# Expert dots of five blocks split between VectorE and ScalarE, a two-pass output projection, and one more row buffer for block 2, on one Trainium2 core

## The chip, the cores and the metric

The kernel runs on one core of a Trainium2 chip: TensorE for matrix products, VectorE and ScalarE for elementwise work, GpSimd, which here only issues gathers, and SyncE, which issues the plain DMAs. The metric is the time of one launch on the device in microseconds. The kernel before takes 3988.34 us, the median of 3 runs from 3983.55 to 3989.04.

## The reference, cut to what matters

One block of a model over 1024 tokens of width 1024, all in float32: a norm, two token mixers (chunked retention and RWKV-7) that are gated, merged and projected by `w_o`, then PEER, a layer of 16384 experts of which every token picks 128, then a gated embedding and a last norm.

```
merged = sigmoid(gate_ret) * branch_ret + sigmoid(gate_rwkv) * branch_rwkv
x  = x + merged @ w_o
h2 = rmsnorm(x, g_ffn)
q  = h2 @ w_pq                      # per head two halves; scores against 128 sub-keys each
ids, gates = top 16 of the sums of the two top-16 lists, for each of 8 heads
act = gelu(sum over d of h2[t, d] * expert_u[ids[t, k], d])      # the "dots"
x  = x + sum over k of gates[t, k] * act[t, k] * expert_v[ids[t, k]]
```

## The kernel before, in words

The 1024 tokens are 8 blocks of 128. The phases have letters, which stand at the start of every name in the profile: M (branches), O (output projection), N (second norm), F (queries and scores), S (choice of the experts), D (dots), K and W (weights for the values), V (values), G (values by gathering), L (the last layer). The number behind the letter is the block, or, for M, O, N and F, a unit of tokens: unit 2 is the last 512 tokens, blocks 4 to 7.

**Dots (D), `dots`, L930 to L972.** For each of a block's 128 choices GpSimd gathers one row of `expert_u` for each token, a tile of 128x1024 floats (L954), and VectorE multiplies it in place with `h2` and sums it, in one instruction with an accumulator (L956). The tile comes from a ring (`row`, L975). Blocks 0 to 2 have `nu` = 3 tiles; from block 3 on `nmore` = 3 tiles of the pool `um` come beside them, 6 in all. A gather waits until the instruction that used its tile last has ended.

**Values.** Blocks 0 to 5 don't gather `expert_v`: all of `expert_v` is streamed through TensorE twice (units V0 and V1, three blocks each), against a matrix of weights M that is built from the choices. A group of 16 tokens of M takes one-hot tiles A (on ScalarE, L1122 and L1123, or on VectorE, L1115, in turn) and B (VectorE, L1128 and L1131), products on TensorE (L1085) and a copy on ScalarE (L1087). Half of the experts (k = 0, then k = 1) is built at a time, 24 groups; the groups of the next half are built beside the stream of the present one. Blocks 6 and 7 gather rows of `expert_v` (L1000), which VectorE adds up (L1002); these take tiles of the same ring.

**Output projection and norm of unit 2 (O2, N2).** `w_out` (L754) loads `w_o` in 16 pieces, four for each quarter of the columns, and multiplies them with all four blocks. `norm2` (L777) takes the four blocks one after the other: sum of squares on ScalarE (L314), a row tile of which there is one (its weights loaded by L788, its product on VectorE by L789, its store by L790), and a scaling (L791). Only then do transposes (L795) and the split into two tiles (L797, L798) follow, and F2.

**Order.** The whole program is written as a list of phases (`order` and `later` in `cfg`, L862). A scheduler turns it into one fixed list of instructions for each engine, with waits by semaphores; it orders by program order and by its own estimate of when things are ready. So an engine that waits for one instruction holds back all that stands behind it, and a change at one place can move instructions of other phases.

## Time and profile before

| | |
|---|---|
| median of 3 runs | 3988.34 us (3983.55 to 3989.04) |
| the profiled execution | 3982.74 us, span 3980.8 us |
| busy, share of the span | TensorE 86%, VectorE 75%, GpSimd 39%, ScalarE 27% |
| granted TensorE clock, mean | 0.922 of 2.4 GHz |
| HBM | 1055.87 MB moved, 265 GB/s in the mean |

The busy shares are means over stages of different kinds. Up to some 1640 us mixers, projections and the dots of blocks 0 and 1 alternate. From there to 2100 us unit 2 is projected, normed and scored while the rows of block 2 come in. From 2100 to 3810 us the dots of blocks 3 to 7, the values and their weights run side by side, and the last 171 us are the last layer. "Granted clock" is the share of TensorE's full speed that the throttle allowed; DMA share is the mean busy share of the 16 DMA engines.

### The profile page before, as it was taken

Reading aid. Unit: us, or ns where it says so; the run is one execution under the profiler, and the core shown is the slowest. Engines: PE = TensorE matmul, PEld = TensorE weight load, DVE = VectorE, ACT = ScalarE, POOL = GpSimd, SP = SyncE. Lnnn points to the kernel's source line nnn. Section 1 sums busy time; section 2 is a strip of 40 time slices with the busy share of each in tenths; the row PEclk is TensorE's granted clock in tenths of the full one; section 3 lists DMA queues with packets and bytes.
Section 4 is the critical chain, followed back from the end, with each engine's and each line's share of the span. In section 5 each row is a group of like instructions: output and inputs, shape, how many; then the busy total and the mean of one; then the engine's idle time right before and its main releaser. Section 6 shows DMA issues by size and latency. Waiting matters only on the chain.

```text
span 3980.8 us, 53073 instructions
## 1 busy us (share of the span) xinstructions
PE 3431.2 (86%) x18323; PEld 2516.6 (63%) x18323; DVE 2974.2 (75%) x7197; ACT 1062.5 (27%) x2232; POOL 1545.5 (39%) x1288
## 2 busy tenths in 40 slices
PE   6997758997899998948568989489898999799988
PEld 6886647887888887536454445366775555466643
DVE  5663487886777764876788999989877898867733
ACT  4432342221232213013371024310732222200022
POOL 0000013223333200044426568765066676777700
PEclk9998879998999999979768999699998999899999
DMA  6336558778777627488849999899399999999941
GB/s 193 111 95 195 170 164 258 224 240 268 243 252 244 210 77 246 139 282 284 277 149 350 413 345 368 305 360 382 115 335 372 380 390 380 370 403 407 407 157 51
DMA packets 499394, 1055.87 MB, mean 265 GB/s; under 512 B 41074, under 2 KB 279220, under 8 KB 499124
## 3 DMA queue, kind: packets, MB, share of 16 engines
q0 software_dynamic: 184320, 671.17, 46.6%
q1 hardware_dynamic: 314804, 381.31, 28.3%
q8 instruction: 144, 2.36, 0.2%
q14 instruction: 126, 1.03, 0.1%
HBM read 990.58 MB, written 61.73 MB: 264 GB/s over the span
## 4 chain that ended last, share of the span: by engine, by line
issue 19%; DMA 13%; POOL 12%; DVE 9%; PE 8%; ACT 0%; SPq 0%; POOLq 0%; DVEq 0%; ACTq 0%
DMA G6.u<-in_peer_v_dram,D6.u_ids 2%; POOL D7.u L954 2%; DMA G7.u<-in_peer_v_dram,D7.u_ids 2%; DMA D2.u<-in_peer_u_dram,D2.u_ids 2%; POOL D6.u L954 2%; DMA D3.u<-in_peer_u_dram,D3.u_ids 2%; POOL D2.u L954 2%; POOL G7.u L1000 2%; POOL D4.u L954 2%; DVE D3.u L956 2%; DVE D5.u L956 2%; POOL G6.u L1000 2%; DMA D5.u<-in_peer_u_dram,D5.u_ids 1%; PE D5.acc L1163 1%; PE W1.pw L1085 1%
## 5 line engine op out<-in xcount | busy, mean ns | idle before, releaser
L1163 PE MATMUL D5.acc<-V0.v,M.M 128*128 128x512 f32 x1536 | 695.1, 610 | 2.4 <-ACT M.M L1087 1.8
L1163 PE MATMUL D7.acc<-V1.v,M.M 128*128 128x512 f32 x1536 | 669.1, 598 | 11.1 <-DMA V1.v<-in_peer_v_dram 11.1
L1163 PEld LDWEIGHTS D7.acc<-V1.v,M.M 128*128 128x128 f32 x1536 | 373.1, 244 | 298.2 <-issue 185.0
L1163 PEld LDWEIGHTS D5.acc<-V0.v,M.M 128*128 128x128 f32 x1536 | 372.6, 247 | 270.9 <-issue 173.0
L954 POOL DMA_INDIRECT D0.u<-in_peer_u_dram,D0.u_ids x128 | 132.4, 1035 | 829.9 <-DMA D0.u_ids<-idsd 542.3
L954 POOL DMA_INDIRECT D2.u<-in_peer_u_dram,D2.u_ids x128 | 137.7, 1076 | 527.5 <-DVE S3.ti L846 302.9
L1085 PEld LDWEIGHTS <-W0.A 128*128 128x128 bf16 x2304 | 153.8, 138 | 188.4 <-issue 115.9
L954 POOL DMA_INDIRECT D1.u<-in_peer_u_dram,D1.u_ids x128 | 136.0, 1063 | 249.6 <-DVE D1.u L956 152.6
L954 POOL DMA_INDIRECT D6.u<-in_peer_u_dram,D6.u_ids x128 | 163.4, 1277 | 177.2 <-DVE S7.m L887 80.0
L956 DVE SCALAR_TENSOR_TENSOR D2.u<-D2.u,D2.u_h 128x1024 f32<-128x1024 f32 x128 | 156.4, 1223 | 86.8 <-DMA D2.u<-in_peer_u_dram,D2.u_ids 86.1
L1085 PE MATMUL W0.pw<-W0.B,W0.A 128*128 128x64 bf16 x1920 | 133.9, 242 | 96.0 <-DVE W0.B L1131 76.4
L1002 DVE SCALAR_TENSOR_TENSOR G7.u_x<-G7.u,D7.u_t,G7.u_x 128x1024 f32<-128x1024 f32 x128 | 164.7, 1287 | 54.9 <-DMA G7.u<-in_peer_v_dram,D7.u_ids 46.6
L954 POOL DMA_INDIRECT D4.u<-in_peer_u_dram,D4.u_ids x128 | 182.3, 1424 | 56.2 <-issue 32.6
L1087 ACT COPY M.M<-W1.pw 128x512 f32<-128x512 f32 x96 | 80.4, 838 | 447.2 <-PE W1.pw L1085 447.2
L956 DVE SCALAR_TENSOR_TENSOR D0.u<-D0.u,D0.u_h 128x1024 f32<-128x1024 f32 x128 | 155.9, 1221 | 56.3 <-DMA D0.u<-in_peer_u_dram,D0.u_ids 54.4
L954 POOL DMA_INDIRECT D3.u<-in_peer_u_dram,D3.u_ids x128 | 142.6, 1114 | 140.8 <-DVE D3.u L956 61.4
L956 DVE SCALAR_TENSOR_TENSOR D1.u<-D1.u,D1.u_h 128x1024 f32<-128x1024 f32 x128 | 156.1, 1222 | 54.3 <-DMA D1.u<-in_peer_u_dram,D1.u_ids 52.7
L956 DVE SCALAR_TENSOR_TENSOR D7.u<-D7.u,D7.u_h 128x1024 f32<-128x1024 f32 x128 | 155.8, 1224 | 54.4 <-DMA D7.u<-in_peer_u_dram,D7.u_ids 47.9
L954 POOL DMA_INDIRECT D7.u<-in_peer_u_dram,D7.u_ids x128 | 168.4, 1316 | 60.6 <-issue 31.7
L956 DVE SCALAR_TENSOR_TENSOR D6.u<-D6.u,D6.u_h 128x1024 f32<-128x1024 f32 x128 | 155.3, 1225 | 47.2 <-DMA D6.u<-in_peer_u_dram,D6.u_ids 46.2
L1000 POOL DMA_INDIRECT G7.u<-in_peer_v_dram,D7.u_ids x128 | 168.5, 1317 | 53.4 <-issue 28.3
L954 POOL DMA_INDIRECT D5.u<-in_peer_u_dram,D5.u_ids x128 | 156.0, 1219 | 80.7 <-issue 18.9
(2267 smaller groups left out, 8452.4 us busy)
## 6 DMA issues: line engine op xcount, KB each, us to landing
V0.v<-in_peer_v_dram SPq DMA_DIRECT2D x128, 512.0 KB
V1.v<-in_peer_v_dram SPq DMA_DIRECT2D x128, 512.0 KB
zsd<-Pw256.stage SPq DMA_DIRECT2D x48, 192.0 KB
Pr0.raw<-in_w_in_dram SPq DMA_DIRECT2D x32, 256.0 KB
Pg0.raw<-in_w_in_dram SPq DMA_DIRECT2D x32, 256.0 KB
F0.raw<-in_w_pq_dram SPq DMA_DIRECT2D x32, 256.0 KB
Pr256.raw<-in_w_in_dram SPq DMA_DIRECT2D x32, 256.0 KB
Pg256.raw<-in_w_in_dram SPq DMA_DIRECT2D x32, 256.0 KB
```

The costliest lines, as they stand in the source:

```text
L954: nc.gpsimd.indirect_dma_start(out=u, out_offset=None, in_=table, in_offset=bass.IndirectOffsetOnAxis(ap=ids[:, k:k + 1], axis=0))
L956: V.scalar_tensor_tensor(u, u, 1.0, h2, op0=ALU.mult, op1=ALU.mult, accum_out=act[:, k:k + 1])
L1000: nc.gpsimd.indirect_dma_start(out=u, out_offset=None, in_=table, in_offset=bass.IndirectOffsetOnAxis(ap=ids[:, k:k + 1], axis=0))
L1002: V.scalar_tensor_tensor(x, u, t[:, k:k + 1], x, op0=ALU.mult, op1=ALU.add)
L1085: nc.tensor.matmul(pw[:, t * 64:t * 64 + 64], At[:, h * 8 + t], B[:, part, h * 2 + t // 4, :, t % 4], start=(part == 0), stop=(part == 2))
L1087: nc.scalar.copy(self.order(tl, k)[:, tt], pw.rearrange("p (t i) -> p t i", t=8))
L1163: nc.tensor.matmul(acc[tb][h], w, v[:, h * 512:h * 512 + 512], start=(k == 0 and s == 0 and m == 0), stop=False)
```

## The change

Three things, of which the diff below shows the core.

- From block 3 on (`wideb` = 3) a row is multiplied by `h2` in place on VectorE (new L969), and ScalarE copies the product in place with an accumulator that gives the sum (new L970). Blocks 0 to 2 keep the one instruction.
- For unit 2 `w_out` runs in two passes of 256 tokens, each of which loads all of `w_o`, so 32 pieces are loaded in place of 16. `norm2` transposes and splits two blocks at a time, as soon as both are scaled.
- The ring becomes a list of pools: 3 tiles, one tile (`nmid`) that is opened with the weights' first pool, and thus in time for block 2, and 2 tiles (`nmore`). Block 2 has 4 tiles, blocks 3 to 7 have 6, as before.

```
     def w_out(self, u, mT):
+        xs = []
+        for b0 in range(0, self.cfg["mf"][u][1], T):
+            xs += self.w_out_pass(u, mT[:, :, b0:b0 + T], b0)
+        return xs
+
+    def w_out_pass(self, u, mT, b0):
...
-        t0, n = self.cfg["mf"][u]
+        t0, n = self.cfg["mf"][u][0] + b0, T
...
             V.tensor_scalar(xs[tb], xs[tb], r, None, op0=ALU.mult)
-        for kc in range(8):
-            pt = self.mm()[:, :n]
-            for tb in range(n // 128):
-                nc.tensor.transpose(pt[:, tb * 128:(tb + 1) * 128], xs[tb][:, kc * 128:(kc + 1) * 128], self.ident)
-            g = self.v("g_ffn", kc)
-            nc.scalar.activation(hT[0][:, kc, :], pt, AF.Copy, scale=g)
-            V.scalar_tensor_tensor(hT[1][:, kc, :], pt, g, hT[0][:, kc, :], op0=ALU.mult, op1=ALU.subtract)
+            if tb % 2:
+                tt = slice(tb * 128 - 128, tb * 128 + 128)
+                for kc in range(8):
+                    pt = self.mm()[:, :T]
+                    for j in range(2):
+                        nc.tensor.transpose(pt[:, j * 128:j * 128 + 128], xs[tb - 1 + j][:, kc * 128:kc * 128 + 128],
+                                            self.ident)
+                    g = self.v("g_ffn", kc)
+                    nc.scalar.activation(hT[0][:, kc, tt], pt, AF.Copy, scale=g)
+                    V.scalar_tensor_tensor(hT[1][:, kc, tt], pt, g, hT[0][:, kc, tt], op0=ALU.mult, op1=ALU.subtract)
...
-               wp2=(512, 4, 3), nu=3, nab=3, lag=1, aact=(1, 2), wide=1, hp=(), nmore=3, lb=2, nk=4,
+               wp2=(512, 4, 3), nu=3, nab=3, lag=1, aact=(1, 2), wide=1, hp=(), nmid=1, nmore=2, wideb=3, lb=2, nk=4,
...
-            V.scalar_tensor_tensor(u, u, 1.0, h2, op0=ALU.mult, op1=ALU.mult, accum_out=act[:, k:k + 1])
+            if b < self.cfg["wideb"]:
+                V.scalar_tensor_tensor(u, u, 1.0, h2, op0=ALU.mult, op1=ALU.mult, accum_out=act[:, k:k + 1])
+            else:
+                V.tensor_mul(u, u, h2)
+                nc.scalar.activation(u, u, AF.Copy, accum_out=act[:, k:k + 1])
...
-        more = self.cfg["nmore"] if self.um else 0
-        if k % (self.nu + more) < self.nu:
-            return self.up.tile([P, D], F32, tag="u", name=self.nm("u"), bufs=self.nu)
-        return self.um.tile([P, D], F32, tag="u", name=self.nm("u"), bufs=more)
+        k %= sum(n for _, n in self.places)
+        for pool, n in self.places:
+            if k < n:
+                return pool.tile([P, D], F32, tag="u", name=self.nm("u"), bufs=n)
+            k -= n
...
+        self.places.append((wc.enter_context(self.tc.tile_pool(name="ux", bufs=1, side="right")), self.cfg["nmid"]))
```

The scheduler then orders all engines anew. Three places of its lists matter here.

ScalarE's list in the middle of block 4, first before. W0.A are the one-hot tiles of the weights (x13: 13 instructions alike), W0.pw the products that are copied into M, D4.u the rows of block 4.

```order
L1122 ACTIVATE W0.A_21599<-cpers,K0.neg_17117 128x128 x13
L1123 ACTIVATE W0.A_21599<-W0.A_21599 128x2048
L1087 COPY M.M_17719<-W0.pw_21623 128x512
L1087 COPY M.M_17719<-W0.pw_21649 128x512
L1087 COPY M.M_15600<-W0.pw_21683 128x512
L1122 ACTIVATE W0.A_21735<-cpers,K2.neg_18281 128x128 x2
L1087 COPY M.M_15600<-W0.pw_21709 128x512
```

The same stretch of ScalarE's list now.

```order
L1137 ACTIVATE W0.A_21842<-cpers,K1.neg_17794 128x128
L1102 COPY M.M_15632<-W0.pw_21866 128x512
L970 ACTIVATE D4.u_19946,D4.u_act_19709<-D4.u_19946 128x1024
L1138 ACTIVATE W0.A_21842<-W0.A_21842 128x2048
L970 ACTIVATE D4.u_19950,D4.u_act_19709<-D4.u_19950 128x1024
L970 ACTIVATE D4.u_19954,D4.u_act_19709<-D4.u_19954 128x1024
L970 ACTIVATE D4.u_19958,D4.u_act_19709<-D4.u_19958 128x1024
L970 ACTIVATE D4.u_19962,D4.u_act_19709<-D4.u_19962 128x1024
L1102 COPY M.M_15632<-W0.pw_21892 128x512
L1102 COPY M.M_17777<-W0.pw_21926 128x512
L970 ACTIVATE D4.u_19966,D4.u_act_19709<-D4.u_19966 128x1024
```

The sums of the rows stand between the tiles A and the copies, so a sum waits for the copies ahead of it, which wait for TensorE.

VectorE's list at the end of the output projection of unit 2, first before. O2.x are the four blocks' rows, N2.h the one row tile of the norm, D2.u the rows of block 2, N2.rsq and N2.st small steps of the norm.

```order
L956 SCALAR_TENSOR_TENSOR D2.u_16770,D2.u_act_16715<-D2.u_16770,D2.u_h_3578_16713 128x1024
L789 SCALAR_TENSOR_TENSOR N2.h_3366_15622<-O2.x_3325_15395,N2.st_15608,N2.h_3366_15622 128x1024
L771 TENSOR_TENSOR O2.x_3328_15401<-O2.x_3328_15401,O2.mm_15585 128x256
L791 TENSOR_SCALAR O2.x_3325_15395<-O2.x_3325_15395,N2.st_15608 128x1024
L276 TENSOR_TENSOR F2.wlo_15945<-F2.raw_15943,F2.whi_15944 128x512
```

The first row of the norm now.

```order
L967 SCALAR_TENSOR_TENSOR D2.u_16784,D2.u_act_16774<-D2.u_16784,D2.u_h_3602_16772 128x1024
L778 TENSOR_TENSOR O2.x_3351_15511<-O2.x_3351_15511,O2.mm_15523 128x256
L796 SCALAR_TENSOR_TENSOR N2.h_3382_15657<-O2.x_3325_15395,N2.st_15643,N2.h_3382_15657 128x1024
L329 SCALAR_TENSOR_TENSOR N2.st_15664<-N2.rsq_15667,N2.st_15664 128x1
L967 SCALAR_TENSOR_TENSOR D2.u_16787,D2.u_act_16774<-D2.u_16787,D2.u_h_3602_16772 128x1024
L798 TENSOR_SCALAR O2.x_3325_15395<-O2.x_3325_15395,N2.st_15643 128x1024
L778 TENSOR_TENSOR O2.x_3352_15513<-O2.x_3352_15513,O2.mm_15533 128x256
L326 TENSOR_TENSOR N2.rsq_15667<-N2.st_15664 128x1
```

The first block's row product stood beside the last addition of the projection (L771); now it stands beside the first addition of the second pass (L778), and 7 more additions follow it.

VectorE's list at the end of block 5, first before. S7 is the choice of experts for block 7; sc, tv and ti belong to its first part (top 16 of each half), oh and the names after it to its second.

```order
L956 SCALAR_TENSOR_TENSOR D5.u_20495,D5.u_act_20116<-D5.u_20495,D5.u_h_4154_20114 128x1024
L847 MATCH_REPLACE S7.sc_25205<-S7.tv_25181,S7.sc_25205 128x128
L846 MAX_INDEX S7.ti_25182<-S7.tv_25181,S7.sc_25205 128x8
L956 SCALAR_TENSOR_TENSOR D5.u_20498,D5.u_act_20116<-D5.u_20498,D5.u_h_4154_20114 128x1024
L848 MAX S7.tv_25181<-S7.sc_25205 128x8
L847 MATCH_REPLACE S7.sc_25205<-S7.tv_25181,S7.sc_25205 128x128
```

The last rows of block 5 now.

```order
L969 TENSOR_TENSOR D5.u_20936<-D5.u_20936,D5.u_h_4178_20429 128x1024
L859 MAX_INDEX S7.ti_25625<-S7.tv_25624,S7.sc_25692 128x8
L883 TENSOR_TENSOR S7.oh_25714<-S7.tv_25624 128x8x16
L969 TENSOR_TENSOR D5.u_20940<-D5.u_20940,D5.u_h_4178_20429 128x1024
L883 TENSOR_TENSOR S7.oh_25714<-S7.tv_25624 128x8x16
```

At the last row of block 5 the choice for block 7 is now in its second part; before it was still in its first. Between the first row of block 5 and the last, 33 instructions of S7 stood in the list before and 100 stand there now; between the last row of block 5 and the tenth row of block 6, 133 of S7 and some 15 groups of weights stood before, and 66 and some 12 groups stand there now.

## Rows read from the trace of the kernel before

**Rows 1.** The page: span, and busy time by engine.
```profile
span 3980.8 us, 53073 instructions
PE 3431.2 (86%) x18323; PEld 2516.6 (63%) x18323; DVE 2974.2 (75%) x7197; ACT 1062.5 (27%) x2232; POOL 1545.5 (39%) x1288
```

**Rows 2.** Stretches: length, busy us (instructions) of five engines, clock, DMA share, GB/s.
```profile
1736.00:1787.00 51.00, 7.92 (x32) 6.02 (x33) 35.78 (x84) 12.89 (x27) 21.33 (x17) 0.50 0.88 308
1787.00:1936.00 149.00, 119.02 (x534) 95.78 (x533) 104.20 (x222) 42.93 (x80) 61.92 (x56) 0.90 0.85 272
1936.00:2022.00 86.00, 36.80 (x386) 28.77 (x384) 66.06 (x142) 36.88 (x73) 32.68 (x34) 0.58 0.79 259
...
2100.00:2307.00 207.00, 184.27 (x492) 83.93 (x491) 191.72 (x603) 11.49 (x27) 124.47 (x113) 0.93 0.98 385
2307.00:2543.00 236.00, 199.65 (x1150) 114.40 (x1149) 212.88 (x377) 77.30 (x181) 181.94 (x128) 0.90 0.95 354
...
2784.00:2872.00 88.00, 75.20 (x659) 60.09 (x659) 73.92 (x308) 68.70 (x149) 5.62 (x6) 0.92 0.28 98
2872.00:3121.00 249.00, 235.98 (x1033) 152.52 (x1032) 201.80 (x378) 71.27 (x151) 159.23 (x124) 0.96 0.93 349
...
3575.00:3810.00 235.00, 226.16 (x521) 153.70 (x520) 166.46 (x134) 0.62 (x2) 165.91 (x126) 0.98 1.00 395
```

**Rows 3.** Waits of VectorE and GpSimd, 1736 to 2022 us: total, times, longest.
```profile
DVE D2.u L956 <- DMA D2.u<-in_peer_u_dram,D2.u_ids: 71.9, 65, 3.1
POOL D2.u L954 <- DVE D2.u L956: 134.2, 79, 6.1
```

**Rows 4.** GpSimd's instructions in order of time: gathers of block 2.
```profile
1988.13 0.94 POOL L954 DMA_INDIRECT D2.u<-in_peer_u_dram,D2.u_ids  x1 [1.46 <-DVE D2.u L956]
...
1994.39 0.94 POOL L954 DMA_INDIRECT D2.u<-in_peer_u_dram,D2.u_ids  x1 [1.01 <-DVE D2.u L956]
```

**Rows 5.** SyncE's instructions in order of time: the row tile of the norm.
```profile
1736.48 1.57 SPq L790 DMA_DIRECT2D h2d<-N2.h  x1
...
1751.26 0.34 SPq L790 DMA_DIRECT2D h2d<-N2.h  x1
...
1765.39 0.33 SPq L790 DMA_DIRECT2D h2d<-N2.h  x1
...
1777.15 0.32 SPq L790 DMA_DIRECT2D h2d<-N2.h  x1
```

**Rows 6.** VectorE's instructions in order of time, two rows of block 4.
```profile
2400.62 1.22 DVE L956 SCALAR_TENSOR_TENSOR D4.u<-D4.u,D4.u_h 128x1024 f32<-128x1024 f32 x1
2401.76 0.09 DVE L956 DVE_READ_ACCUMULATOR D4.u<-D4.u,D4.u_h 128x1 f32 x1
2401.76 1.22 DVE L956 SCALAR_TENSOR_TENSOR D4.u<-D4.u,D4.u_h 128x1024 f32<-128x1024 f32 x1
...
2402.90 0.69 DVE L1131 TENSOR_TENSOR W0.B<-W0.one,K0.w 128x1024 bf16<-128x1024 bf16 x1
```

**Rows 7.** Groups: busy us, mean ns, idle before; float32 tiles of 512 and 256 columns.
```profile
L276 DVE TENSOR_TENSOR F2.wlo<-F2.raw,F2.whi 128x512 fp32r<-128x512 f32 x32 | 22.1, 690 | 3.2 <-ACT F2.whi L275 3.1
...
L771 DVE TENSOR_TENSOR O2.x<-O2.x,O2.mm 128x256 f32<-128x256 f32 x16 | 6.7, 422 | 3.5 <-PE O2.mm L296 3.5
```

**Rows 8.** ScalarE's instructions in order of time: a sum of squares.
```profile
1739.25 1.05 ACT L314 ACTIVATE N2.junk<-O2.x 128x1024 bf16<-128x1024 f32 x1
1740.21 0.19 ACT L314 ACTIVATION_READ_ACCUMULATOR N2.junk<-O2.x 128x1 f32 x1
1740.30 0.60 ACT L275 CAST F2.whi<-F2.raw 128x512 fp32r<-128x512 f32 x1
```

**Rows 9.** Waits of ScalarE, first 2307 to 2543 us, then 2872 to 3121 us.
```profile
ACT M.M L1087 <- PE W0.pw L1085: 153.5, 30, 42.1
...
ACT M.M L1087 <- PE W1.pw L1085: 152.5, 15, 37.2
```

**Rows 10.** The page, costliest groups: the stream of the last three blocks' values.
```profile
L1163 PE MATMUL D7.acc<-V1.v,M.M 128*128 128x512 f32 x1536 | 669.1, 598 | 11.1 <-DMA V1.v<-in_peer_v_dram 11.1
```

More of the change, by code (lines that the diff above doesn't have):

```diff
@@ L112, in __init__ @@
         self.kw = {}
-        self.um, self.hT, self.wide = None, {}, 0
+        self.hT, self.wide = {}, 0
         self.ph = "s"
@@ L760, in w_out @@
         for tb in range(n // 128):
-            x = big.tile([P, D], F32, tag=f"x1_{tb}", name=self.nm("x1"))
+            x = big.tile([P, D], F32, tag=f"x1_{b0 // 128 + tb}", name=self.nm("x1"))
             self.q.dma_start(x, self.i["x"][0, t0 + tb * 128:t0 + tb * 128 + 128, :])
@@ L932, in open_dots @@
         self.up = up.enter_context(self.tc.tile_pool(name=self.nm("up"), bufs=1, side="right"))
-        self.nu = n
+        self.places = [(self.up, n)]
         return up
@@ L1019, in open_values @@
         self.vp = e(self.tc.tile_pool(name="vp", bufs=2))
-        if self.cfg["nmore"]:
-            self.um = e(self.tc.tile_pool(name="um", bufs=1))
+        self.places.append((e(self.tc.tile_pool(name="um", bufs=1)), self.cfg["nmore"]))
         self.wide_ctx = ExitStack()
@@ L1224, in last_weights @@
         self.ph = "L"
-        places = [lambda k=k: self.row(k) for k in range(self.nu + self.cfg["nmore"])]
+        places = [lambda k=k: self.row(k) for k in range(sum(n for _, n in self.places))]
         places += [lambda: self.wb.tile([P, D], F32, tag="A", name=self.nm("A"), bufs=self.cfg["nab"])] * 2
```

## The prediction

> **What bounds the kernel now.** I read the page first, then a table of stretches, then who waits in the stretches that the change touches. By the page TensorE is busy for 86% of the span and VectorE for 75%, ScalarE for 27% [rows 1]; no engine is full. The table tells more [rows 2]. From 2100 us on four things are nearly full at once: in block 4 (2307 to 2543 us) VectorE is busy 213 of 236 us, TensorE 200, the DMA engines 95% of the time, and in the last stretch before the tail (3575 to 3810) TensorE 226 of 235 us with the DMA engines at 1.00. So time is lost or won there only where such a stretch starts later or earlier, or in its holes. Two holes stand out. Before 2100 us the rows of block 2 run with three tiles: VectorE waits 71.9 us for rows, and GpSimd 134.2 us for a tile to come free [rows 3]. And from 2784 to 2872 us the DMA engines are at 0.28, since VectorE and ScalarE build weights and choose experts before they take up block 6 [rows 2].
>
> The sums are made against the profiled execution, 3982.74 us (span 3980.8 and 1.9 around it). The median of the three runs, 3988.34, lies 5.6 above it, the lowest 0.8 above; I add 3 at the end.
>
> **The change part by part.**
>
> *Fourth tile for block 2.* A tile's round is a gather, its landing, the product, and the next gather: with three tiles, every third gather starts 1994.39 - 1988.13 = 6.3 us after the one before in the same tile [rows 4], so 2.1 us a row. With four tiles and the same round it would be 1.6 us. VectorE itself needs 1.14 us for a row (start to start) [rows 6] beside its other work. What can be won is what VectorE waits for rows, 71.9 us between 1736 and 2022 us, since behind a waiting row its list also holds back the splits of F2 and the tiles B. What limits it: the DMA engines are at 0.88, 0.85 and 0.79 in these three stretches [rows 2], though at no more than 308 GB/s, where 395 GB/s go through at 1.00 later. Bounds: 0 (no room in the transfers) and -72. I take a little over half: **-40**.
>
> *Projection and norm in halves.* The norm has one row tile, and its four stores start at 1736.5, 1751.3, 1765.4 and 1777.2 us [rows 5], some 13.6 us apart; TensorE is busy only 7.9 of the 51 us until F2 starts [rows 2]. Two of these four rounds now come before the projection's end. All of it would be 2 x 13.6 = 27 us. But VectorE's list still holds 14 rows of block 2 between the last addition and the last split of the norm, where it held 16, so the rows set the pace here, too. From these 51 us I take 15 off, with the rows' own gain in the term above. Against it stand 16 more loads of 256 KB, 4.2 MB, at 308 GB/s 13.6 us of transfers beside a DMA share of 0.88; of these I count 8. Bounds -27 and +14; I take **-7**.
>
> *What the new order moves.* Up to the first row of block 4, 52 more instructions of S4 and S5 stand in VectorE's list after block 2 (31 and 21), and about a group more of the second half's tiles. Work in S steps is short, some 0.2 us each by the spacing of the trace; 52 x 0.2 = 10, and 8 tiles of 0.6 us (0.69 us, as the B in [rows 6], less the overlap with the next) 5: **+15**, on the path, since VectorE is busy 192 of 207 us in block 3. The work comes back at the end of block 5: 67 instructions of S7 (13 us) and 3 of 15 groups of weights stand no longer between block 5 and 6. This hole lasts 88 us, with ScalarE busy 69 of them [rows 2]; 3 of 15 groups are 14 us of ScalarE's 69. S7 hides partly behind it. I take **-17**, bounds -30 and 0, and **+3** for the S7 now between the rows of block 5.
>
> *Product and sum.* On VectorE nothing is won: the accumulator's readout shows 0.09 us, but the next instruction starts at the same moment as the readout, 1.14 us after the row's start [rows 6]. Products of two float32 tiles take 422 ns for 256 columns and 690 for 512 [rows 7], so 1.05 ns a column and, carried on, 690 + 536 = 1226 ns for 1024, where the old instruction takes 1.22 us. If the readout counted after all, 5 x 128 x 0.09 = 58 us of VectorE would go; that is the far end. The Trainium skill (Vector Engine (DVE) Microarchitecture Reference, "Points that are easy to get wrong") says that the old form of instruction runs at half throughput when its two sources lie in SBUF and are not bf16. By that alone the split would halve VectorE's time for a row, an estimate of half a microsecond for each of 640 rows, 320 us. The trace disagrees, since the old instruction on two float32 sources takes no longer than a plain product would [rows 6, 7], and this way gets no chance.
>
> On ScalarE a sum over 1024 columns holds the engine from 1739.25 to 1740.30: 1.05 us [rows 8], 134 us a block. The Trainium skill (Vector Engine (DVE) Microarchitecture Reference, "Points that are easy to get wrong") says that the old instruction runs at half rate when both its sources are in SBUF and not bf16; it would then take over 2.1 us and the split would save a microsecond a row, some 640 us in all. The trace has 1.22 us for two float32 sources and disagrees, so this result gets no chance.
>
> What it costs is a longer round for each tile (one more engine, at least 1.05 us) and ScalarE's list. In block 4 ScalarE is busy 77.3 of 236 us; with 134 it is 211, which leaves 25. In block 6 it is 71.3 + 134 = 205 of 249. And it waits for TensorE's products, 153.5 us in 30 waits in block 4, 152.5 in 15 in block 6 [rows 9]. Such waits cost nothing before; now a row's sum stands behind them, behind the sum the tile, and behind the tile GpSimd's next gather. If a quarter of the waits can't be filled with sums, block 4 takes 211 + 38 = 249 us, 13 more; block 6 stays at 205 + 38 = 243, below its 249, and I put 5 on it; for the longer round in blocks 3, 5 and 7, whose transfers are full anyway, 4 each. Sum **+30**; bounds -58 (readout counted) and +84 (half of the waits stay: 211 + 77 = 288, +52, and 205 + 76 = 281, +32). The Trainium skill (ScalarE: Activation LUTs, "Rules for kernel authors") would leave simple adds and products on VectorE, which speaks against this part. The trace agrees in so far as VectorE gets nothing back for ScalarE's 134 us a block [rows 6, 8]; what following the rule would save is the second rival's price, told below from rows.
>
> Sum: -40 - 7 + 15 - 17 + 3 + 30 = **-16**. 3982.7 - 16 + 3 = **3970 us**, 0.46% below the median. The term for the hole and that for block 2 reach the end because the end is fixed by the rows: after the weights of the last half are done, TensorE streams that half, 669.1/2 = 335 us [rows 10], and the rows of block 7 keep the transfers at 1.00 up to the same moment [rows 2]; a stretch of rows that starts earlier ends earlier.
>
> **The rivals.** A difference under 0.2% (8 us) can't be told from none here: 3980 to 3996 is "same".
>
> - *All of block 2's waits go and the hole shrinks in full*: -72 and -30 in place of -40 and -17: 3925 us. For it: 395 GB/s are possible, 308 are used. Against: the loads of F2 beside the rows. Chance 0.16.
> - *ScalarE's list sets the pace of the rows.* The place is block 4, then 6: copies wait for TensorE, sums behind them, and the ring of six runs dry. Half of the waits left gives +84 in place of the +30, with the rest of it: 3970 + 54 = 4024 us. It decides from the point where ScalarE's part costs over 54 us, which eats up the other terms (-46) and 8 more. For it: 25 us are left free of 236, 153.5 of waits. Against: TensorE has idle time in block 4, so the copies are due soon after the tiles B. Chance 0.25.
> - *The fourth tile is hidden by the transfers*: VectorE's waits go on because the DMA engines are full, 15 in place of 40: 3995 us, no change. For it: shares of 0.79 to 0.88, and 4.2 MB more. Chance 0.15.
>
> **How the numbers follow.** The forecast has 0.44; its own range is 3945 to 3983, of which 0.04 lie in "same". Faster: 0.40 + 0.16 = 0.56. Same: 0.04 + 0.15 = 0.19. Slower: 0.25. The range goes from 3920, below the first rival, to 4015, which holds the milder half of the second: 0.8.
>
> **What would show it.** Right: block 2's last row lands near 1975 us instead of 2021, with VectorE's waits for rows at about half; the product at about 1.22 us and 1.14 from start to start; ScalarE's sum at 1.05; block 4 between 236 and 260 us; the hole before block 6 near 70 us. Wrong: GpSimd waiting for ScalarE by tens of microseconds in blocks 4 and 6, F2 starting no earlier than 1787 us, a hole of 88 us, or block 3 growing by more than 15 us.

## The result, and the profile after

The changed kernel takes 4044.75 us, the median of 4 runs (4041.04 to 4062.50), against 3988.03 for the kernel before in the same comparison: 1.0153 times as long, 95% interval 1.0122 to 1.0185. Forecast were 3970 us, in a range from 3920 to 4015. The profiled execution has a span of 4039.3 us, 58.5 more than before.

The first line of the page's table of busy time (answers to [rows 1]): ScalarE alone has more to do, 1766.6 us against 1062.5; the others are where they were.

```profile
PE 3431.9 (85%) x18323; PEld 2517.9 (62%) x18323; DVE 2969.4 (74%) x6565; ACT 1766.6 (44%) x3520; POOL 1557.6 (39%) x1288
```

Block 2, its gathers and its dots (count, ns min/median/max, first and last start), and the dots before. The last dot starts at 1977.2 us, where it was 2020.5: the fourth tile does its work, and VectorE's wait for rows (total, times, longest) is 46.4 us, where it was 71.9 [rows 3].

```profile
L964 POOL DMA_INDIRECT D2.u<-in_peer_u_dram,D2.u_ids x128: 932/938/1944, 1650.8 to 1971.5; - x128
L967 DVE SCALAR_TENSOR_TENSOR D2.u<-D2.u,D2.u_h x128: 1211/1225/1285, 1681.4 to 1977.2; 128x1024 f32<-128x1024 f32 x128
DVE D2.u L967 <- DMA D2.u<-in_peer_u_dram,D2.u_ids: 46.4, 49, 6.2
...
L956 DVE SCALAR_TENSOR_TENSOR D2.u<-D2.u,D2.u_h x128: 1203/1225/1276, 1681.6 to 2020.5; 128x1024 f32<-128x1024 f32 x128
```

The stretches behind it in the changed kernel, cut at the blocks' ends, with the columns of [rows 2]: the choice of experts and the weights ahead of block 3, blocks 3, 4 and 5, the hole, block 6.

```profile
1979.00:2100.00 121.00, 97.52 (x913) 71.26 (x914) 101.21 (x340) 106.63 (x224) 37.15 (x24) 0.78 0.37 128
2100.00:2309.00 209.00, 174.79 (x430) 77.55 (x429) 184.97 (x426) 132.63 (x238) 131.55 (x105) 0.91 0.95 361
2309.00:2548.00 239.00, 188.03 (x1169) 111.28 (x1168) 213.08 (x253) 213.91 (x439) 164.65 (x129) 0.89 0.93 342
2548.00:2794.00 246.00, 190.50 (x722) 134.61 (x720) 219.47 (x512) 174.07 (x332) 154.33 (x129) 0.88 0.93 349
2794.00:2880.00 86.00, 71.26 (x528) 55.16 (x529) 69.28 (x233) 65.85 (x143) 13.45 (x9) 0.88 0.35 116
2880.00:3157.00 277.00, 239.18 (x1162) 159.61 (x1161) 190.40 (x230) 210.36 (x409) 160.93 (x123) 0.91 0.82 309
```

The 43 us of block 2 are gone by the end of block 3 (2309 against 2307 us). Blocks 4 and 5 are 3 and 5 us longer. The hole is as long as it was (86 against 88 us), and block 6 takes 277 us in place of 249, with the DMA engines at 0.82 in place of 0.93 and the granted clock at 0.91 in place of 0.96, both means between its two levels (0.50 is 1.2 GHz, 1.00 is 2.4) [rows 2].

Who waits there: GpSimd, for ScalarE's sums, in block 3, in block 4, and from the hole to block 6's end (total, times, longest).

```profile
POOL D3.u L964 <- ACT D3.u L970: 142.4, 96, 40.6
...
POOL D4.u L964 <- ACT D4.u L970: 42.6, 51, 2.3
...
POOL D6.u L964 <- ACT D6.u L970: 164.0, 81, 65.0
```

The rows tell only half of it. Cut the same time by what TensorE works on: first the weights of V0 with the stream of its first half, up to the last product of W0; then V0's second half with the first weights of V1; then the rest of V1. Columns as above; first after, then before.

```profile
1994.00:2602.00 608.00, 464.27 (x2670) 267.28 (x2669) 533.99 (x1069) 489.17 (x971) 362.96 (x282) 0.85 0.83 305
2602.00:3053.00 451.00, 399.60 (x1745) 287.37 (x1743) 355.17 (x796) 320.16 (x620) 220.18 (x181) 0.94 0.76 288
3053.00:3870.00 817.00, 759.03 (x2895) 461.11 (x2894) 614.49 (x558) 313.99 (x627) 545.91 (x429) 0.96 0.96 372
```

```profile
2023.00:2602.00 579.00, 481.19 (x2714) 278.46 (x2713) 526.19 (x1249) 182.39 (x410) 371.99 (x290) 0.87 0.87 327
2602.00:3008.00 406.00, 381.88 (x1699) 275.74 (x1699) 348.35 (x1022) 119.72 (x258) 196.71 (x165) 0.97 0.80 300
3008.00:3811.00 803.00, 759.03 (x2896) 460.42 (x2894) 632.98 (x764) 118.77 (x270) 568.32 (x443) 0.97 0.99 388
```

TensorE starts 29 us earlier and needs 29, 45 and 14 us more: 59 us later at the end. In the second and third stretch of before it is busy 382 of 406 and 759 of 803 us; this is the engine that is nearly full from 2602 us to the end. Its waits after, in the first, the second and the third stretch:

```profile
PE W0.pw L1100 <- ACT W0.A L1138: 87.7, 12, 17.7
...
PE K5.pw L1069 <- DMA K5.raw<-wd: 23.1, 1, 23.1
PE W1.pw L1100 <- ACT M.M L1102: 18.2, 3, 6.9
...
PE W1.pw L1100 <- ACT M.M L1102: 41.2, 6, 13.4
```

All of them end on ScalarE or on block 5's late end; before they were 17.7, 12.8, 0.2 and 0 us. They are not all new time, since before TensorE waited for VectorE's tiles B in the first and in the third stretch, and did so for 26.4 and 0 us after:

```profile
PE W0.pw L1085 <- DVE W0.B L1131: 76.4, 26, 13.8
...
PE W1.pw L1085 <- DVE W1.B L1131: 32.7, 2, 22.1
```

### The profile page after: what moved, and what is told of

Its sections match the earlier page's. It is cut to its first block, busy times and chain, and to the rows that moved or that the text cites. A ratio compares the mean times of both kernels' runs of the same rounds, so it can differ in the third digit from the quotient of the medians.

```text
span 4039.3 us, 54176 instructions
## 1 busy us (share of the span) xinstructions
PE 3431.9 (85%) x18323; PEld 2517.9 (62%) x18323; DVE 2969.4 (74%) x6565; ACT 1766.6 (44%) x3520; POOL 1557.6 (39%) x1288
## 3 DMA queue, kind: packets, MB, share of 16 engines
q14 instruction: 135, 1.11, 0.1%
## 4 chain that ended last, share of the span: by engine, by line
issue 20%; POOL 16%; DMA 10%; PE 7%; DVE 5%; ACT 3%; POOLq 0%; SPq 0%; DVEq 0%; ACTq 0%
POOL D3.u L964 3%; POOL D6.u L964 3%; DMA G7.u<-in_peer_v_dram,D7.u_ids 3%; POOL D7.u L964 2%; POOL G6.u L1015 2%; POOL D2.u L964 2%; POOL D4.u L964 2%; DMA G6.u<-in_peer_v_dram,D6.u_ids 1%; POOL G7.u L1015 1%; POOL D5.u L964 1%; PE D5.acc L1178 1%; DMA D4.u<-in_peer_u_dram,D4.u_ids 1%; DMA D2.u<-in_peer_u_dram,D2.u_ids 1%; DMA D5.u<-in_peer_u_dram,D5.u_ids 1%; DMA D6.u<-in_peer_u_dram,D6.u_ids 1%
## 5 line engine op out<-in xcount | busy, mean ns | idle before, releaser
L964 POOL DMA_INDIRECT D6.u<-in_peer_u_dram,D6.u_ids x128 | 172.5, 1347 | 189.5 <-ACT D6.u L970 164.0
L964 POOL DMA_INDIRECT D3.u<-in_peer_u_dram,D3.u_ids x128 | 168.7, 1318 | 160.0 <-ACT D3.u L970 142.4
L969 DVE TENSOR_TENSOR D6.u<-D6.u,D6.u_h 128x1024 f32<-128x1024 f32 x128 | 155.5, 1225 | 85.7 <-DMA D6.u<-in_peer_u_dram,D6.u_ids 78.6
L969 DVE TENSOR_TENSOR D7.u<-D7.u,D7.u_h 128x1024 f32<-128x1024 f32 x128 | 156.0, 1224 | 67.2 <-DMA D7.u<-in_peer_u_dram,D7.u_ids 52.9
L1100 PE MATMUL W1.pw<-W1.B,W1.A 128*128 128x64 bf16 x2304 | 149.9, 243 | 59.7 <-ACT M.M L1102 59.4
L1100 PEld LDWEIGHTS <-W1.A 128*128 128x128 bf16 x2304 | 148.0, 138 | 80.7 <-issue 77.1
L964 POOL DMA_INDIRECT D4.u<-in_peer_u_dram,D4.u_ids x128 | 164.5, 1285 | 75.0 <-ACT D4.u L970 42.6
L964 POOL DMA_INDIRECT D7.u<-in_peer_u_dram,D7.u_ids x128 | 159.1, 1243 | 82.6 <-ACT D7.u L970 56.7
```

The costliest lines, as they stand in the source:

```text
L964: nc.gpsimd.indirect_dma_start(out=u, out_offset=None, in_=table, in_offset=bass.IndirectOffsetOnAxis(ap=ids[:, k:k + 1], axis=0))
L969: V.tensor_mul(u, u, h2)
L1100: nc.tensor.matmul(pw[:, t * 64:t * 64 + 64], At[:, h * 8 + t], B[:, part, h * 2 + t // 4, :, t % 4], start=(part == 0), stop=(part == 2))
```

## The experiments

Ratios are to the kernel before, run beside each group, with 95% intervals. The times of different groups are not compared with each other, only their ratios, and a per cent is 40 us.

**Each part undone or alone.** The split taken back: `wideb=3` becomes

```
wideb=8
```

> The changed kernel with its old instruction for the dots of all eight blocks (product and sum in one on VectorE); fourth tile and halves stay. Theory A: the split alone is what costs; the fourth tile and the halves keep the 43 us by which block 2 ended earlier in the changed kernel (1977 against 2020 us). Then 3988 - 43 = 3945 us, between 3930 and 3960, block 3 again some 211 us in earnest, and nobody waits for ScalarE's sums. Rival B: the new order of the instructions (more of S4 and S5 before block 4) and the halves cost the time; then it stays at 4020 or above, with block 2's early end lost again in block 3.

Measured: 3971.32 us, 0.9972 [0.9954, 0.9990]. Rival B falls: the split is what costs, 1.8% or some 72 us. But theory A's 43 us are not there either; 11 are.

The split alone, in the kernel before:

```
-            V.scalar_tensor_tensor(u, u, 1.0, h2, ..., accum_out=act[:, k:k + 1])
+            if b < 3:
+                V.scalar_tensor_tensor(u, u, 1.0, h2, ..., accum_out=act[:, k:k + 1])
+            else:
+                V.tensor_mul(u, u, h2)
+                nc.scalar.activation(u, u, AF.Copy, accum_out=act[:, k:k + 1])
```

> The kernel before with the split of blocks 3 to 7 alone; three tiles in block 2, projection and norm whole. Theory A: the split costs 57 + 43 = 100 us, so about 4085 us, between 4060 and 4100, with GpSimd waiting for ScalarE over 100 us in blocks 3 and 6. Rival B: 3985 to 4005 us, about as before.

Measured: 4067.17 us, 1.0228 [1.0209, 1.0247]: some 91 of theory A's 100 us, and inside its range. GpSimd waits 131.9 us for ScalarE's sums in block 3 and 159.6 in block 6, as A has it. So the split costs some 20 us more here than beside the other two parts.

The fourth tile taken back: `nmid=1, nmore=2` becomes

```
nmore=3        # and no pool "ux"
```

> The changed kernel without the fourth tile (three tiles in block 2, three more from block 3's end on as before); split and halves stay. Theory A: block 2 ends some 35 to 43 us later again and nothing gives it back: 4080 us, between 4065 and 4095. Rival C: what block 2 wins is lost behind it in any case, because the rows of block 3 wait for the weights of the first half on ScalarE; then it stays within 10 us of 4045.

Measured: 4072.76 us, 1.0254 [1.0231, 1.0277], theory A. So beside the split the fourth tile is worth 40 us with the halves (1.0254 against the changed kernel's 1.0153) and 17 without them (1.0228 for the split alone, 1.0186 in the next run).

Projection and norm whole again (`w_out` and `norm2` of the kernel before; the edit cut to its core):

```
-        for b0 in range(0, self.cfg["mf"][u][1], T):
-            xs += self.w_out_pass(u, mT[:, :, b0:b0 + T], b0)
+        t0, n = self.cfg["mf"][u]       # one pass; the transposes stand behind all four blocks again
```

> The changed kernel with projection and norm of the last 512 tokens whole again; fourth tile and split stay. Theory A: a few us, as the prediction's term of 7: 4045 to 4060 us. Rival: the second read of the projection's weights (4.2 MB) costs more than the earlier norm gives; then 4030 to 4044.

Measured: 4050.89 us, 1.0186 [1.0162, 1.0209]; the changed kernel's interval overlaps. The pairs of runs with and without halves lie up to 0.33% apart, in both signs (-0.33% for this one, +0.26% for the split with three tiles): what the halves are worth stays open, within some 0.3%.

The fourth tile alone in the kernel before, which is the changed kernel with the split and the halves taken back:

```
-  nmore=3
+  nmid=1, nmore=2, wideb=8
```

> The kernel before with the fourth tile for block 2 alone (old instruction throughout, projection and norm whole). With the halves as well it was 0.28% faster than before. Theory A: what block 2 wins is not what TensorE waits for; its tiles B stand still further behind in VectorE's list (row 45 of block 5 for the last group of V0's second half, against 22 before): no change, 3975 to 3990 us. Rival (the rows fix the end): some 30 us faster, 3950.

Measured: 3976.86 us, 0.9986 [0.9963, 1.0008]. No change that can be told, although block 2's dots end 34 us earlier (1986.8 us): theory A.

**What fixes the end.** Half of G7's rows left out of the kernel before:

```
-                self.fetch(128)
+                self.fetch(64)          # and 64 rows in direct() for the last block
```

> The kernel before with 64 of the 128 rows of the last direct gather, G7 (the last block's output lacks half of its sum). Theory A: TensorE's list fixes the end, since it was busy 226 of 235 us beside G7: only the 9 us in which it idled there, 8 to 11 us of waits for V1's tiles, can go: 3970 us, within 8. Rival, the prediction's step (the end is fixed by the rows): 64 x 1.7 us earlier, bounded by the last tiles of V1: 3900 us or below.

Measured: 3974.81 us, 0.9989 [0.9970, 1.0007]. 64 rows less, and the time stays. TensorE's stream of V1 hardly moves, where G7's last addition starts 116 us earlier. First before, then with half of the rows:

```profile
L1163 PE MATMUL D7.acc<-V1.v,M.M x1536: 592/592/1226, 3038.5 to 3810.1; 128*128 128x512 f32 x192
L1002 DVE SCALAR_TENSOR_TENSOR G7.u_x<-G7.u,D7.u_t,G7.u_x x128: 1283/1285/1351, 3582.7 to 3795.9; 128x1024 f32<-128x1024 f32 x128
...
L1164 PE MATMUL D7.acc<-V1.v,M.M x1536: 592/593/1202, 3035.0 to 3794.3; 128*128 128x512 f32 x192
L1003 DVE SCALAR_TENSOR_TENSOR G7.u_x<-G7.u,D7.u_t,G7.u_x x64: 1283/1285/1347, 3574.2 to 3680.2; 128x1024 f32<-128x1024 f32 x64
```

The stream's end is 16 us earlier in a profiled execution of 3966.85 us, 8 below the median of its ten. The rows do not fix the end, TensorE's list does. All twenty traces agree: the span ends 163 to 166 us behind TensorE's last product for the last three blocks or behind G7's last addition, whichever ends later. In eighteen of them this is TensorE's product, by 19 us in the kernel before and 31 in the changed one. The other two are the next two runs. The counter-test gives TensorE's work a better place, with the old instruction:

```
-  later=("D3 S4 D4 S5 D5", "S6 S7 G6 G7")
+  later=("D3 S4 D4", "S6 S7 G6 G7"), mid="S5 D5"
...
+            if i == 1:
+                self.later(self.cfg["mid"])
```

> The changed kernel with the old instruction throughout, and block 5 (its choice and its rows) written behind the weights of V0's second half, so that the tiles B of the last group stand at row 101 of block 4 in VectorE's list and not at row 39 of block 5. Theory A: TensorE takes up V0's second half some 60 us earlier, and what it then waits for are the groups of V1's first half, the last of which stand at row 51 of block 6 and not at 62: 11 rows of 2 us and some of TensorE's idle time, 3945 us, between 3925 and 3960. Rival (the rows fix the end): no change, 3971 us within 10, since block 5 is not earlier.

Measured: 3945.22 us, 0.9916 [0.9889, 0.9943]: the one version that beats both kernels clearly. Its three stretches of TensorE, and the last gathers:

```profile
1991.00:2488.00 497.00, 460.01 (x2682) 267.25 (x2679) 450.31 (x1004) 180.44 (x402) 323.68 (x248) 0.95 0.87 333
2488.00:2933.00 445.00, 411.24 (x1931) 298.75 (x1930) 400.17 (x1259) 133.75 (x287) 203.57 (x178) 0.95 0.79 297
2933.00:3700.00 767.00, 735.09 (x2691) 444.95 (x2690) 603.62 (x756) 104.59 (x246) 548.83 (x429) 0.98 0.99 389
```

```profile
L1015 POOL DMA_INDIRECT G7.u<-in_peer_v_dram,D7.u_ids x128: 932/1020/1996, 3538.2 to 3763.2; - x128
```

The first stretch is 497 us in place of 579 (the second is 39 us longer, the third 36 shorter), TensorE ends V1 at 3700 us, and now the rows come last: the bound has changed sides, which is why only 37 us of the 110 that TensorE wins there show in the time. Against the same kernel in the old order (0.9972, 0.9979) the order alone gives 0.6%.

With the split in this order:

> The changed kernel with its split, and block 5 written behind the weights of V0's second half, as in the run at 3945 us, which had the old instruction. Theory A: with TensorE ahead, the rows set the end, and they are longer by ScalarE's sums in blocks 3 and 5 to 6, some 40 to 60 us: 3985 to 4005 us. Rival (the split costs only through TensorE's list): 3945 to 3960 us.

Measured: 4036.56 us, 1.0139 [1.0113, 1.0166], 2.2% above the run without the split. Theory A has the direction and half of the size; the rival falls. G7's last gather starts at 3862.7 us and not at 3763.2, and TensorE is done with V1 a hundred us before the rows. So the split costs whichever list sets the end. In the changed kernel itself G7's last addition starts at 3842.8 us, 47 later than before, and later than TensorE's last product there (3815.2): by an estimate from these two, the rows alone would have ended it some 28 us later than before.

**Where the split costs.** In blocks 5 and 6 alone, and in 3, 4 and 7 alone:

```
-            if b < self.cfg["wideb"]:
+            if b not in (5, 6):         # the other run: (3, 4, 7)
```

> The changed kernel with the split in blocks 5 and 6 alone, the old instruction elsewhere. Compared with the old instruction throughout, TensorE's stretch between the last weight of V0's second half and V1's start was 55 us longer with the split (451 against 396 us), the stretches before and behind it 6 us each. Theory A (the cost sits where TensorE's list has little else, that is in blocks 5 and 6): 3971 + 55 = 4026 us, between 4010 and 4035. Rival (each of the five blocks costs the same, 15 us): 4000 us.

> The changed kernel with the split in blocks 3, 4 and 7 alone, the old instruction elsewhere. Theory A: 3971 + 12 = 3983 us, between 3970 and 3995. Rival (each block the same): 3971 + 45 = 4016 us. Rival (ScalarE's weights A for V0 wait in block 4, where it is busy 214 of 239 us): over 4010 us with the stretch up to V0's last weight over 620 us long.

Measured: 4020.61 us, 1.0097 [1.0059, 1.0135], and 3987.23 us, 1.0018 [0.9999, 1.0038]. Against 0.9972 that is 50 and 18 us, together 68 of the whole split's 72, as theory A had both. Two blocks carry three quarters.

**What of the split costs.** ScalarE's sums left out, so that the activations of blocks 3 to 7 are zeros:

```
-                nc.scalar.activation(u, u, AF.Copy, accum_out=act[:, k:k + 1])
```

> The changed kernel without ScalarE's sums: the product stays on VectorE, the activations of blocks 3 to 7 are zeros in place of the dots (one memset a block). Theory A: ScalarE's sums are all that the split costs, and the product takes VectorE as long as the old instruction: 3971 us as with the old instruction throughout, within 15. Rival: VectorE's pitch falls by the 0.09 us of the readout, 58 us of VectorE's time; then below 3945.

Measured: 4016.30 us, 1.0106 [1.0065, 1.0147]; neither theory. Nothing waited for block 5's rows any more, and the scheduler drew nine groups of V1's tiles B in among them (behind rows 65 to 127), where the other kernels have two. This run tells of the order and not of the sums, and was replaced by the one with the old instruction on each block's last row:

```
+            if b < self.cfg["wideb"] or k == 127:
                 V.scalar_tensor_tensor(...)
```

> The changed kernel without ScalarE's sums, as in the run without sums, but with the old instruction for the last row of each of the blocks 3 to 7, so that the block's weights depend on its last row again (the other 127 activations are zeros). In VectorE's list the tiles B stand within three rows of where the old instruction throughout has them, which they did not in the run without sums. Theory A: the product costs VectorE what the old instruction did: 3971 us, within 12. Rival 1: the readout counted, 58 us of VectorE less: below 3945. Rival 2: a plain product is worse for the rows than the old instruction (its neighbours, the gathers): 4000 us or above, as in the run without sums.

Measured: 3989.09 us, 1.0028 [1.0005, 1.0051]: between theory A and rival 2. The sums shortened:

```
-                nc.scalar.activation(u, u, AF.Copy, ...)
+                nc.scalar.activation(u[:, :64], u[:, :64], AF.Copy, ...)
```

> The changed kernel with ScalarE's sum over the first 64 of the 1024 columns (the dots are sums of 64 products): every sum stays in ScalarE's list behind its product and holds its tile until then, but holds the engine for some 0.25 us in place of 1.05 us. Theory A1 (occupation: 640 x 1.05 us in ScalarE's list delay the tiles A and the copies that TensorE waits for): 3971 to 3990 us. Rival A2 (dependence: what counts is that copies stand behind sums that wait for rows, and rows behind sums): 4020 us or above.

Measured: 4002.52 us, 1.0054 [1.0032, 1.0075]: between A1 and A2. Three steps that are each a fraction of a per cent need one comparison, so the old instruction, the products without sums and the short sums were run again side by side, in this order.

> The changed kernel with the old instruction throughout, beside the next two on one chip. Theory A: 0.997 of before, between 0.995 and 0.999.

> The products of blocks 3 to 7 without ScalarE's sums, the old instruction on each block's last row. Theory A (the product costs VectorE what the old instruction did; the 0.56% between the two kernels came from two chips): within 0.3% of the old instruction throughout. Rival (the product itself costs some 20 us): 0.4 to 0.7% slower than it.

> ScalarE's sums over 64 of 1024 columns. Theory A (what a sum that waits in ScalarE's list costs, without its length): 0.6 to 1.0% slower than the old instruction throughout, and the rest up to the changed kernel's 1.0153 is the sums' length. Rival (the length is all): within 0.3% of the products without sums.

Measured: 3969.21 us, 0.9979 [0.9961, 0.9996]; 3988.01 us, 1.0021 [1.0002, 1.0039]; 4008.47 us, 1.0078 [1.0055, 1.0101]. Theory A holds for the first, the rival for the second, and A for the third. So the product without any sum costs 0.42% (17 us) against the old instruction, a short sum that waits in ScalarE's list 0.57% more (23 us), and its full length 0.75% more up to the changed kernel's 1.0153 (30 us, this last step across two comparisons). The steps were taken in this one order; what the product would cost beside the sums is not shown. Nor did a run move the sums, at their number and length, behind the copies in ScalarE's list, which would test directly that their place there is what TensorE waits for.

**What differs beside a product at the same pitch.** GpSimd's gathers show a difference. In the changed kernel one lasts 13.97 us, where from 1640 us on the median is 1.11 and all but eight take less than 2.05; beside it, VectorE's list in the same 14 us (start, us, engine, line, operation):

```profile
2949.04 1.20 POOL L964 DMA_INDIRECT D6.u<-in_peer_u_dram,D6.u_ids  x1 [0.65 <-ACT D6.u L970]
2951.80 13.97 POOL L964 DMA_INDIRECT D6.u<-in_peer_u_dram,D6.u_ids  x1 [1.57 <-ACT D6.u L970]
2966.07 0.94 POOL L964 DMA_INDIRECT D6.u<-in_peer_u_dram,D6.u_ids  x1 [0.30 <-issue]
```

```profile
2951.95 1.22 DVE L969 TENSOR_TENSOR D6.u<-D6.u,D6.u_h 128x1024 f32<-128x1024 f32 x1
2953.09 0.76 DVE L1143 TENSOR_TENSOR W1.one<-iotag,K3.ij 128x512 bf16<-128x512 bf16 x2
...
2960.78 0.77 DVE L1143 TENSOR_TENSOR W1.one<-iotag,K5.ij 128x512 bf16<-128x512 bf16 x2
2961.45 3.50 DVE L969 TENSOR_TENSOR D6.u<-D6.u,D6.u_h 128x1024 f32<-128x1024 f32 x3
```

VectorE has no gap from 2951.95 to 2964.95, nothing but tensor-tensor instructions, and the gather ends 0.8 us behind the last. This is no rule for every gather: the one at 2949.04 starts in the same run of instructions without a gap and takes 1.20 us. In the changed kernel 103 gathers start beside such a run of tensor-tensor instructions with 2.5 us or more of it to come; 3 were held over 2.2 us, the others took at most 1.97. What decides between them was not found, so the expectation below, that such a gather lasts 4 to 14 us, says too much. With the old instruction (the run at 0.9979) a gather held beside such tiles ends 0.88 us after the first accumulator readout begins:

```profile
1989.99 8.74 POOL L964 DMA_INDIRECT D3.u<-in_peer_u_dram,D3.u_ids  x1 [0.30 <-issue]
```

```profile
1996.70 1.21 DVE L967 SCALAR_TENSOR_TENSOR D3.u<-D3.u,D3.u_h 128x1024 f32<-128x1024 f32 x1
1997.85 0.07 DVE L967 DVE_READ_ACCUMULATOR D3.u<-D3.u,D3.u_h 128x1 f32 x1
1997.85 0.74 DVE L1143 TENSOR_TENSOR W0.one<-iotag,K1.ij 128x512 bf16<-128x512 bf16 x2
```

Gathers over 2.2 us between 1640 us and the end: none before, 4 (22 us in all) in the run with the old instruction at 0.9979, 16 (87 us) with the products at 1.0021, 8 (49 us) in the changed kernel. The four with the old instruction come with the new order, as the fourth tile alone has five (19 us). Two runs ask whether the form of the product or the missing readout does it:

```
-                V.tensor_mul(u, u, h2)
+                V.scalar_tensor_tensor(u, u, 1.0, h2, op0=ALU.mult, op1=ALU.mult)
```

> The products of blocks 3 to 7 without ScalarE's sums, as in the second of the three runs on one chip (1.0021 of before), but made by the old instruction without its accumulator; the lists are in the same order. In the traces so far a gather of GpSimd that falls beside an unbroken run of VectorE's tensor-tensor instructions lasts 4 to 14 us in place of 0.93, and none did in the kernel before, where each row ends with a readout of the accumulator; with the products there were 16 over 2.2 us in blocks 3 to 7, 86 us in all, and with the old instruction 4, 22 us in all. Theory A (the readout is what lets GpSimd in): as with the products, 1.002 of before, some 16 long gathers. Rival (the form of the product keeps GpSimd out): 0.998 of before, some 4 long gathers.

> The changed kernel with its product made by the old instruction without the accumulator, in the same order, ScalarE's sums as they are. Theory A (the readout lets GpSimd in): as the changed kernel, 1.0153 of before, long gathers in blocks 3 and 6 (8 with 49 us in the changed kernel). Rival (the form of the product): some 0.4% less, 1.011, and hardly a long gather.

Measured: 3985.73 us, 1.0022 [1.0005, 1.0040], with 17 long gathers (91 us); and 4057.46 us, 1.0194 [1.0169, 1.0219], with 5 (43 us). The old instruction without its accumulator behaves as the product does, so it is the accumulator with its readout that spares the gathers, not the form of the product. (The second run lies 0.4% above theory A's figure, across two comparisons; why is open.) The six traces of kernels with the old instruction throughout agree: no gather was held past a readout. That the held gathers are the 17 us was not isolated, and their sum does not follow the time: the changed kernel has fewer than the products alone, and is slower.

The Trainium skill (SBUF — State Buffer, "Who interferes with whom") says that a VectorE instruction with two inputs in SBUF contends with GpSimd instructions that read it, and adds, as inferred, that descriptor generation for DMAs is spared by `tensor_tensor`. The trace agrees with the first, since a gather reads its row numbers from a tile in SBUF (`D6.u_ids`) and can be held beside nothing but tensor-tensor instructions, 25 of them in a row. Whether the descriptors are spared, no run here separates.

## Why the prediction was wrong, point by point

- *"The end is fixed by the rows; a stretch of rows that starts earlier ends earlier"*: this is the step that failed, and with it the gains it was to pass on. Block 2 ended 43 us earlier, as forecast (1977 for 1975), and at the end 8 to 11 us of it were left with halves and new order (0.9979, 0.9972), 6 without halves, not told from none. TensorE was busy 226 of 235 us in the last stretch [rows 2], and the prediction read this as rows and TensorE that end at the same moment, and added up gains of the rows alone. In the runs TensorE ends 19 us behind the rows in the kernel before, and with half of G7 left out, which ends the rows 116 us earlier, the time does not move. What moves it is TensorE's list: 110 us earlier there, with rows that are 25 us earlier, gave 37.
- *New order, +15*: on VectorE's side it came out: from block 2's last dot to block 3's there are 297 us in the run at 0.9979 and 285 before, 12 more. What reaches the end is another part of the order, the tiles B: in VectorE's list the last group of V0's second half stands behind row 39 of block 5 in the run at 0.9979, behind row 22 before. TensorE's first stretch lasts 602 us there in place of 579, so 23 of the 25 us by which it starts earlier (1998 for 2023) go there.
- *The hole, -17*: 86 us in place of 88, or 80 when it is cut where VectorE takes its rows up again (2872.4 us), as the 88 are. With the old instruction and the new order (0.9979) it is 73 us long, from block 5's last dot at 2748 us to 2821, so the term came out there. But 14 more tiles B and 79 more instructions of S7 stand among the rows of block 6 then, which takes 265 us in place of 249: hole and block 6 together are as long as before (338 for 337), and this the term left out. In the changed kernel GpSimd also waits 65 us of the hole for one sum; its product was ready at 2804.3 us, and it stands in ScalarE's list behind the tiles A and copies of V1's weights:

```profile
L967 DVE SCALAR_TENSOR_TENSOR D6.u<-D6.u,D6.u_h x128: 1203/1224/1295, 2820.6 to 3085.5; 128x1024 f32<-128x1024 f32 x128
...
2866.01 3.02 ACT L1137 ACTIVATE W1.A<-cpers,K3.neg 128x128 bf16<-128x128 f32 x10
2868.93 1.05 ACT L970 ACTIVATE D6.u<-D6.u 128x1024 f32<-128x1024 f32 x1
...
2870.33 1.69 POOL L964 DMA_INDIRECT D6.u<-in_peer_u_dram,D6.u_ids  x1 [65.05 <-ACT D6.u L970]
```

VectorE's own list has its next product only at 2872.4 us, so this wait alone does not explain the hole's length.
- *Product and sum, +30*: the term mis-sized most. It is 69 us: 17 for the product, 23 for sums that wait, 30 for their length. The pitch was right (three products in 3.50 us, 1.14 from start to start), the sum's 1.06 us too, and block 4 came out at 239 us, below the 249. Block 3 was put at +4; from block 2's last dot to its own it takes 330 us, 33 more than with the old instruction. Block 6 was put at +5; with the hole it takes 364 us, 26 more than with the old instruction. There the prediction compared ScalarE's work (205 us) with the block's length (249) and left out that TensorE, full from 2602 us on, waits for the copies that stand behind the sums.
- *The second rival* (ScalarE's list sets the rows' pace, 4024 us) is what happened, at a place it named second, and too small: its price was set on GpSimd's and VectorE's side alone. Of the prediction's signs of being wrong, GpSimd's waits of tens of microseconds for ScalarE came in blocks 4 and 6, and the longest total in block 3. TensorE's second stretch alone is 57 us longer than in the run at 0.9979 (451 against 394): 19 more busy, at a clock of 0.94 in place of 0.98, and 38 more idle. In the run at 0.9979 the first two stretches are:

```profile
1998.00:2600.00 602.00, 481.45 (x2707) 278.52 (x2705) 544.33 (x1304) 181.44 (x405) 403.97 (x301) 0.85 0.86 324
2600.00:2994.00 394.00, 380.54 (x1704) 276.07 (x1702) 344.31 (x1019) 119.86 (x258) 216.38 (x162) 0.98 0.81 305
```

- *Halves, -7*: F2's first product starts at 1782.5 us, 5 earlier than before, and its last at 1912.6, 20 earlier. Between runs that differ by the halves alone the first product is 10 us earlier with them (1782.5 for 1792.4 beside the split, 1784.6 for 1794.7 without it) and the last 8 to 10. (The fourth tile alone has the first 7 us later than the kernel before, the last 9 earlier.) What that is worth at the end was not settled.
- *The two estimates that it refused*: the prediction works the same rule out twice, once to 320 us and once to 640. No run bears out either, since the pitch stayed at 1.14 us.

With what was measured the sum reads: fourth tile, halves and order -8, split +69, so +61, where the medians differ by 57. The 69 are the difference of the same two ratios, so that this closes is no further proof. The parts are not independent either: without the other two the split costs 91.

## What to carry to other kernels

Before a term is added to a sum, ask which engine's list is full from there to the end: in this kernel 34 us won for the rows were worth nothing that could be told, while moving one phase behind TensorE's weights gave 0.6%. An engine at 27% is not free to take work if its list holds what a full engine waits for; price the new work by who waits behind it, on both sides. And compare busy share with length for each engine that reads or feeds the moved work, not only for the one that gets it.

## What the runs showed of the hardware that was not expected

A gather on GpSimd that starts beside an unbroken run of VectorE's tensor-tensor instructions can be held until that run ends and some 0.8 us more (13.97 us at most in the changed kernel, where the median is 1.11). Most are not: 3 of 103 in the changed kernel, and what decides it is open. An accumulator readout, which costs VectorE nothing in pitch [rows 6], ended the hold wherever one came, in the six traces of kernels with the old instruction throughout. So one fused instruction with an accumulator is friendlier to GpSimd's gathers than the plain product of the same duration: 4 long gathers against 16, in nearly the same order of instructions.
